# Row norms in groups, scaled in place and stored a tile later, between the mixers and the out-projection of a hybrid encoder on one Trainium2 core

## The chip, the core and the metric

The kernel runs on one core of a Trainium2 chip. The metric is the device time in microseconds (us) of one execution. The core's engines are TensorE (PE in the profile, with PEld for its weight loads), VectorE (DVE), ScalarE (ACT), GpSimd (POOL) and SyncE (SP, which issues most of the DMAs). Each engine runs its own list of instructions in order, and waits where an instruction needs something of another engine or of a DMA.

## The reference

A layer of an encoder: a norm, one projection whose columns go to four mixers, an out-projection with a residual, then a mixture of sixteen experts and a gate. The lines that matter here, cut:

```python
def rmsnorm(x, w):
    xf = x.astype(jnp.float32)
    y = xf * lax.rsqrt(jnp.mean(xf * xf, axis=-1, keepdims=True) + EPS)
    return (y * w.astype(jnp.float32)).astype(x.dtype)
...
def mamba2_mixer(...):
    ...
    y = (y_f + y_b + xs * d_skip[:, None]).reshape(nb, L, GROUP_W)
    return rmsnorm(y * jax.nn.silu(z), norm_w)
...
def hyena_mixer(...):
    ...
    return rmsnorm(y * x0, norm_w)
...
        mixed = jnp.concatenate([retention_mixer(...), mamba2_mixer(...),
                                 hyena_mixer(...), gdn_mixer(...)], axis=-1)
        h = h + jnp.einsum('bln,nd->bld', mixed, w_out[i])
        h = h + expert_choice_moe(rmsnorm(h, norm_ffn_w[i]), router_w[i], ...)
        gate = jax.nn.sigmoid(jnp.einsum('bld,de->ble', rmsnorm(h, ple_norm_w[i]), ple_gate_w[i]))
        h = h + gate * jnp.einsum('blk,kd->bld', p[i], ple_proj_w[i])
    return rmsnorm(h, final_norm_w)
```

SEQ is 1024, D_MODEL 1024, and each mixer gives 256 columns (GROUP_W). All arrays are float32.

## The kernel before

The sequence is worked in eight tiles of 128 tokens (partitions), and in this part of the program from tile 7 down to tile 0. First come the in-projection and the four mixers; then the out-projection and the routing; then sixteen experts, whose weights stream from memory the whole time.

Products are made in three parts: a float32 tile is split into a rounded high part and the rest. For weights, `chunk` loads a block of 128x1024 into `raw`, makes `wh` (the high part, on ScalarE, L1617 or L1620) and `wl` (what is left, by a subtraction, L1618 or L1622). Chunks 1 and 2 of the out-projection's weights also carry the norm weights of the state-space and hyena mixers (L1617, L1618, on VectorE); chunks 0 and 3 do not, and their subtraction (L1622) is put on GpSimd by `pool=c in (0, 3)`. For activations, `rows_T` transposes a tile on TensorE (L1635, tile `tk`), copies the high part on ScalarE (L1636, `xh`) and subtracts on VectorE (L1637, `xl`). `mm3` then issues three matmuls for each pair (L1646 to L1648, tile `ga`). `rw` holds the router's weights, which eight GpSimd instructions scale by a norm weight (L1673).

The end of the mixers is three lists of steps that `weave` interleaves:

- Retention, `attend` and `finish`, a tile ahead of each other: ScalarE's queue loads `rr` (L1445, two buffers), VectorE makes `rqh` (L1447, one buffer), TensorE transposes both (L1451, L1456), ScalarE copies them (L1453 `rqk_`, L1458 `rqt`), TensorE multiplies (L1464 scores, L1468 and L1469 outputs), VectorE masks the scores (L1465, `rS`). `finish` centres and scales the heads: sums and means on VectorE (L1475, L1476, L1478), squares on ScalarE (L1480), a sum (L1481), the root on GpSimd (L203, L204, `rgs`), then L1483, and L1485 writes the result into `rU`, which stays in on-chip memory. The load of `rr` of one tile goes into the buffer of the tile two before, which L1485 of that tile reads last.
- The state-space mixer: `combine` makes `sy` (two buffers): L1061 and L1064 on GpSimd, L1064, L1065 and L1068 on VectorE.
- Hyena: `y` holds all eight tiles; L1393 makes the last product of each.

The rows of `sy` and of `y` are normed by `norm_store`, one tile at a time: a square with its sum on ScalarE (L1086, into `njk`), the root on GpSimd (L203, L204, `nss`, 128x1), a scaling from `y` into `njk` on ScalarE (L1088), and a store of `njk` to the DRAM array MX (L1089), issued from ScalarE's queue. `njk` has two buffers. The out-projection loads 768 columns of a tile back from MX (tile `a`).

Tiles come from pools. `sb2` holds the tiles of the state-space mixer and retention; when it is closed, `sb3`, with the out-projection's `wl3`, `a4`, `xh` and `xl`, opens where it lay, and a tile waits for the tile whose place it takes (`reuse_waits="tile"`). The tile `w4`, which takes the high part of chunk 3, lies where hyena's `y` lay. The order of instructions on each engine is set by a list scheduler with a timeline of its own, not by the order in the source.

## Time and profile before

| | us |
|---|---|
| runs | 1656.79, 1653.63, 1647.57 |
| median of the runs | 1653.63 |
| profiled execution | 1651.48 |
| its span, first to last instruction | 1649.6 |
| PE / DVE / ACT / POOL busy in the span | 1513.7 / 1195.3 / 862.2 / 559.0 |

The mean granted TensorE clock is 0.959 of its upper level of 2.4 GHz. Times in the rows count from the span's start. An engine's busy share is an average over stages with different limits, so the rows below go by stages: the mixers end and the out-projection begins between 690 and 740 us, the out-projection runs to some 860 us, and the experts follow.

### The profile page before, as it was taken

Reading aid. Unit: us, or ns where it says so; the run is one execution under the profiler, and the core shown is the slowest. Engines: PE = TensorE matmul, PEld = TensorE weight load, DVE = VectorE, ACT = ScalarE, POOL = GpSimd, SP = SyncE. Lnnn points to the kernel's source line nnn. Section 1 sums busy time; section 2 is a strip of 40 time slices with the busy share of each in tenths; the row PEclk is TensorE's granted clock in tenths of the full one; section 3 lists DMA queues with packets and bytes.
Section 4 is the critical chain, followed back from the end, with each engine's and each line's share of the span. In section 5 each row is a group of like instructions: output and inputs, shape, how many; then the busy total and the mean of one; then the engine's idle time right before and its main releaser. Section 6 shows DMA issues by size and latency. Waiting matters only on the chain.

```text
span 1649.6 us, 25979 instructions
## 1 busy us (share of the span) xinstructions
PE 1513.7 (92%) x9148; PEld 1251.9 (76%) x9148; DVE 1195.3 (72%) x2060; ACT 862.2 (52%) x1413; POOL 559.0 (34%) x778
## 2 busy tenths in 40 slices
PE   4999999999999899779997999999898999999997
PEld 4877778988778776568875787886676688787886
DVE  5589876942556477955778797998888887777673
ACT  6255342123444335433223776887776767676662
POOL 3126665672865068462223110111111021121121
PEclk9999999999999899869997999999999999999999
DMA  5213557454545485154345999999999988888771
GB/s 182 61 39 96 168 155 243 131 161 105 166 122 167 139 288 163 55 181 156 135 154 214 359 337 363 317 339 350 349 355 336 348 294 295 293 310 303 236 276 52
DMA packets 200671, 362.53 MB, mean 220 GB/s; under 512 B 62046, under 2 KB 124732, under 8 KB 200285
## 3 DMA queue, kind: packets, MB, share of 16 engines
q1 hardware_dynamic: 169016, 296.13, 52.2%
q0 software_dynamic: 12400, 42.29, 8.5%
q10 hardware_dynamic: 19125, 22.45, 4.0%
q8 instruction: 72, 1.18, 0.3%
q14 instruction: 58, 0.48, 0.1%
HBM read 301.04 MB, written 59.77 MB: 219 GB/s over the span
## 4 chain that ended last, share of the span: by engine, by line
PE 45%; DMA 18%; DVE 17%; issue 8%; POOL 6%; ACT 5%; SPq 0%; POOLq 0%; ACTq 0%; DVEq 0%
PE pj L300 8%; DVE wl L1622 6%; PE pj L318 5%; PE ga L1646 4%; DMA raw<-in_exp_w_gate_dram 4%; PE ga L1648 4%; PE ga L1647 4%; DMA raw<-in_exp_w_up_dram 3%; ACT wh L1620 2%; POOL prm L1208 2%; POOL prr L1208 2%; PE pj L1647 2%; PE pj L1646 2%; PE pj L1648 2%; DMA RT<-mo 2%
## 5 line engine op out<-in xcount | busy, mean ns | idle before, releaser
L1622 DVE TENSOR_TENSOR wl<-raw,wh 128x1024 fp32r<-128x1024 f32 x340 | 408.3, 1223 | 86.2 <-ACT wh L1620 83.6
L1620 ACT CAST wh<-raw 128x1024 fp32r<-128x1024 f32 x344 | 356.4, 1052 | 139.1 <-DMA raw<-in_exp_w_up_dram 46.1
L1647 PE MATMUL ga<-wl,xh 128*128 128x512 f32 x512 | 206.4, 403 | 6.8 <-DVE wl L1622 6.7
L1648 PE MATMUL ga<-wh,xl 128*128 128x512 f32 x480 | 189.8, 396 | 0.0
L1646 PE MATMUL ga<-wh,xh 128*128 128x512 f32 x480 | 177.2, 407 | 10.0 <-ACT wh L1620 9.7
L1647 PEld LDWEIGHTS ga<-wl,xh 128*128 128x128 f32 x512 | 98.1, 192 | 34.7 <-DVE wl L1622 15.9
L318 PE MATMUL pj<-wh,hnh 128*128 128x256 f32 (+1 forms) x384 | 113.0, 295 | 7.9 <-DVE zss L915 4.6
L300 PE MATMUL pj<-hnh,wh 128*128 128x512 f32 x288 | 118.4, 411 | 0.8 <-ACT cin L337 0.8
L1646 PEld LDWEIGHTS ga<-wh,xh 128*128 128x128 f32 x480 | 90.6, 191 | 34.9 <-ACT wh L1620 16.5
L300 PE MATMUL pj<-hnl,wh 128*128 128x512 f32 x288 | 117.0, 406 | 0.0
L2009 POOL DMA_INDIRECT H<-b,pidx x15 | 35.4, 2357 | 240.6 <-ACT b L2008 213.7
L300 PE MATMUL pj<-hnh,wl 128*128 128x512 f32 x288 | 116.7, 405 | 0.0
L318 PE MATMUL pj<-wl,hnh 128*128 128x256 f32 (+1 forms) x384 | 110.5, 288 | 0.0
L318 PE MATMUL pj<-wh,hnl 128*128 128x256 f32 (+1 forms) x384 | 110.5, 288 | 0.0
L1647 PE MATMUL pj<-wl,hh 128*128 128x512 f32 x256 | 103.8, 406 | 4.1 <-DVE wl L1622 4.1
L1648 PEld LDWEIGHTS ga<-wh,xl 128*128 128x128 f32 x480 | 91.8, 191 | 18.1
L1648 PE MATMUL pj<-wh,hl 128*128 128x512 f32 x256 | 100.1, 396 | 0.0
L1956 POOL DMA_INDIRECT a<-HN,pidx x16 | 29.9, 1871 | 200.0 <-PE pj L1647 66.4
L1646 PE MATMUL pj<-wh,hh 128*128 128x512 f32 x256 | 89.9, 397 | 0.2 <-ACT hh L1636 0.2
L318 PEld LDWEIGHTS pj<-wh,hnh 128*128 128x128 f32 x384 | 74.4, 194 | 10.4 <-issue 4.1
L346 DVE SCALAR_TENSOR_TENSOR cacc<-cin,pcolh,cacc 128x1024 f32<-128x1024 f32 x48 | 64.8, 1349 | 15.6 <-POOL prm L1208 7.0
L318 PEld LDWEIGHTS pj<-wl,hnh 128*128 128x128 f32 x384 | 74.3, 193 | 0.5 <-issue 0.3
(540 smaller groups left out, 3751.6 us busy)
## 6 DMA issues: line engine op xcount, KB each, us to landing
raw<-in_exp_w_down_dram SPq DMA_DIRECT2D x128, 512.0 KB
raw<-in_exp_w_gate_dram SPq DMA_DIRECT2D x108, 512.0 KB
raw<-in_exp_w_up_dram SPq DMA_DIRECT2D x104, 512.0 KB
wraw<-in_w_in_dram SPq DMA_DIRECT2D x30, 512.0 KB
g<-WD SPq DMA_DIRECT2D x16, 768.0 KB
room<-in_exp_w_up_dram SPq DMA_DIRECT2D x24, 512.0 KB
WD<-gB SPq DMA_DIRECT2D x16, 640.0 KB
room<-in_exp_w_gate_dram SPq DMA_DIRECT2D x18, 512.0 KB
```

What stands on the lines that cost most here:

```text
L300: self.on_pj = nc.tensor.matmul(pj, lhsT=A[:, kt], rhs=B[:, kt, hs], start=i == 0, stop=i == 23)
L318: self.on_pj = nc.tensor.matmul(pj, lhsT=A[:, kt, ts], rhs=B[:, kt, :], start=i == 0, stop=i == 23)
L346: nc.vector.scalar_tensor_tensor(acc, cin[:, 2 - r + j:2 - r + j + 1024], w[j], acc, op0=OP.mult, op1=OP.add)
L1208: tt = lambda o, a, b, op: nc.gpsimd.tensor_tensor(out=o, in0=a, in1=b, op=op)
L1620: nc.scalar.copy(h, r)
L1622: e.tensor_tensor(out=l, in0=r, in1=h.bitcast(F32), op=OP.subtract)
L1646: nc.tensor.matmul(ps, lhsT=xh[:, k], rhs=wh[:, hs], start=first, stop=False)
L1647: nc.tensor.matmul(ps, lhsT=xh[:, k], rhs=wl[:, hs], start=False, stop=False)
L1648: return nc.tensor.matmul(ps, lhsT=xl[:, k], rhs=wh[:, hs], start=False, stop=last)
L1956: self.fetched = self.nc.gpsimd.indirect_dma_start(out=xg, out_offset=None, in_=self.HN if src is None else src, in_offset=bass.IndirectOf ...
L2009: nc.gpsimd.indirect_dma_start(out=self.H, out_offset=bass.IndirectOffsetOnAxis(ap=idx[:, :1], axis=0), in_=y, in_offset=None, compute_op= ...
```

## The change

Three things are changed.

**The norms.** `norm_store` becomes two steps. `norms(ys)` squares a group of rows into `njk` (only as a place to put the squares), and takes one root for the group on GpSimd. `store` then scales a row in place, in `y` or `sy` itself, and issues its store to MX from there. The state-space mixer calls `store` for a tile after the next tile has been combined; hyena groups its tiles as (7, 6), (5, 4, 3, 2), (1, 0), with a `yield` between the norms and the stores of a group. `nss` has four buffers and not two.

**The subtractions.** `pool=c in (0, 3)` is dropped, so that the weight subtractions of chunks 0 and 3 run on VectorE too. The eight scalings of `rw` become one instruction on VectorE over 128x128.

**The places.** The tiles `sbT`, `smv`, `sxb`, `sdec`, `sST` are the first to be laid into `sb2`, and `wl3`, `a4`, `xh`, `xl` the first into `sb3`.

```diff
+    def pcs(self, name, n):
+        j = self.col[name]
+        return self.PC[:, j:j + n]
...
     def ssm(self):
         nc, a = self.nc, self.a
         T2 = self.t2
+
+        T2([128, 256], "sbT", 2)
+        T2([128, 4, 128], "smv", 3)
+        T2([128, 4, 128], "sxb", 2)
+        T2([128, 4, 64], "sdec")
+        ST = T2([128, 8, 4, 2, 64], "sST")
...
-        ST = T2([128, 8, 4, 2, 64], "sST")
...
-            self.norm_store(y, t, 256)
-
-        E = weights(NT - 1)
+            return self.norms([y]), 0, y, t, 256
+
+        E, made = weights(NT - 1), None
         for t in range(NT - 1, -1, -1):
             if t < NT - 1:
                 backward(t)
             p = products(t)
             En = weights(t - 1) if t else None
-            combine(t, E, *p)
+            done, made = made, combine(t, E, *p)
+            if done:
+                self.store(*done)
             E = En
             yield
-
-    def norm_store(self, y, t, col):
-
-        nc = self.nc
-        s = self.t4([128, 2], "nss", 2)
-        jk = self.t4([128, 256], "njk", 2)
-        nc.scalar.activation(jk, y, AF.Square, accum_out=s[:, 0:1])
-        self.rsqrt(s[:, 1:2], s[:, 0:1], 1.0 / 256, EPS)
-        nc.scalar.activation(jk, y, AF.Copy, scale=s[:, 1:2])
-        nc.scalar.dma_start(self.MX[t][:, col:col + 256], jk)
-
+        self.store(*made)
+
+    def norms(self, ys):
+
+        nc = self.nc
+        n = len(ys)
+        s = self.t4([128, 2, 4], "nss", 4)
+        for i, y in enumerate(ys):
+            jk = self.t4([128, 256], "njk", 2)
+            nc.scalar.activation(jk, y, AF.Square, accum_out=s[:, 0, i:i + 1])
+        self.rsqrt(s[:, 1, 0:n], s[:, 0, 0:n], 1.0 / 256, EPS)
+        return s
+
+    def store(self, s, i, y, t, col):
+
+        nc = self.nc
+        nc.scalar.activation(y, y, AF.Copy, scale=s[:, 1, i:i + 1])
+        nc.scalar.dma_start(self.MX[t][:, col:col + 256], y)
...
-        for t in range(NT - 1, -1, -1):
-            nc.vector.tensor_tensor(out=y[:, t], in0=y[:, t], in1=x0[(7 - t) // 2][:, t % 2], op=OP.mult)
-            self.norm_store(y[:, t], t, 512)
+        for ts in ((7, 6), (5, 4, 3, 2), (1, 0)):
+            for t in ts:
+                nc.vector.tensor_tensor(out=y[:, t], in0=y[:, t], in1=x0[(7 - t) // 2][:, t % 2], op=OP.mult)
+            s = self.norms([y[:, t] for t in ts])
+            yield
+            for i, t in enumerate(ts):
+                self.store(s, i, y[:, t], t, 512)
             yield
...
         w = {}
+
+        for n, dt, bufs in (("wl3", F32R, 6), ("a4", F32, 2), ("xh", F32R, 2), ("xl", F32R, 2)):
+            self.t3([128, 1024], n, bufs, dt=dt)
...
-            w[c] = self.chunk(a["w_out"][0], c, pool=c in (0, 3), norm=(None, "ssm_norm_w", "hy_norm_w", None)[c],
+            w[c] = self.chunk(a["w_out"][0], c, norm=(None, "ssm_norm_w", "hy_norm_w", None)[c],
                               first=2 * c, **own)
         rw = self.t5([128, 8, NE], "rw")
         nc.sync.dma_start(rw, a["router_w"][0].rearrange("(k p) e -> p k e", p=128))
-        for k in range(8):
-            nc.gpsimd.tensor_scalar(rw[:, k], rw[:, k], self.pc("norm_ffn_w", k), None, op0=OP.mult)
+        nw8 = self.pcs("norm_ffn_w", 8)
+        nc.vector.tensor_tensor(out=rw, in0=rw, in1=nw8[:, :, None].to_broadcast([128, 8, NE]), op=OP.mult)
```

The scheduler turns this into another order on the engines. The lists below are the instruction lists of both kernels at three places; the line numbers after are those of the new source (L1447 of before is L1469 after, L1465 is L1487, L1481 is L1503, L1618 is L1640, L1622 is L1644, L1637 is L1659).

VectorE, at the end of the mixers, before:

```order
731 L1485 TENSOR_TENSOR rU<-ro,rr 128x256
732 L1465 TENSOR_TENSOR rS<-sp,rdm 128x2x128 x2
733 L1618 SCALAR_TENSOR_TENSOR wl_7057<-raw_7055,pcol,wh_7056 128x1024
734 L1618 SCALAR_TENSOR_TENSOR wl_7063<-raw_7061,pcol,wh_7062 128x1024
735 L1618 SCALAR_TENSOR_TENSOR wl_7081<-raw_7079,pcol,wh_7080 128x1024
736 L1618 SCALAR_TENSOR_TENSOR wl_7087<-raw_7085,pcol,wh_7086 128x1024
737 L1447 TENSOR_TENSOR rqh<-rr,rpw 128x512
738 L1475 TENSOR_REDUCE rgs<-sp 128x4
739 L1476 TENSOR_SCALAR rgs<-rgs 128x4
740 L1478 TENSOR_TENSOR ro<-sp,rgs 128x256
741 L1637 TENSOR_TENSOR xl<-tk,xh 128x512
```

and after:

```order
732 L1469 TENSOR_TENSOR rqh<-rr,rpw 128x512
733 L1500 TENSOR_TENSOR ro<-sp,rgs 128x256
734 L1640 SCALAR_TENSOR_TENSOR wl_7050<-raw_7048,pcol,wh_7049 128x1024
735 L1640 SCALAR_TENSOR_TENSOR wl_7056<-raw_7054,pcol,wh_7055 128x1024
736 L1644 TENSOR_TENSOR wl_7062<-raw,wh_7061 128x1024
737 L1644 TENSOR_TENSOR wl_7068<-raw,wh_7067 128x1024
738 L1640 SCALAR_TENSOR_TENSOR wl_7074<-raw_7072,pcol,wh_7073 128x1024
739 L1640 SCALAR_TENSOR_TENSOR wl_7080<-raw_7078,pcol,wh_7079 128x1024
740 L1503 TENSOR_REDUCE rgs<-sp 128x4
741 L1698 TENSOR_TENSOR rw<-rw,pcol 128x128
742 L1644 TENSOR_TENSOR wl_7085<-raw,w_7043 128x1024
743 L1644 TENSOR_TENSOR wl_7090<-raw,w_7043 128x1024
```

Before, `rqh` and the steps L1475 to L1478 follow the four subtractions L1618, and the first `xl` follows them directly; after, `rqh` and the steps come first, then six subtractions, L1503, the scaling of `rw`, two more subtractions, and then `xl`.

GpSimd, at the last tile of the state-space mixer (`rgs` is the root of retention, `nss` of the norms), before:

```order
456 L1061 TENSOR_TENSOR sy<-sxT,dsk 128x256
457 L1064 TENSOR_TENSOR sy<-sy,sy_6986 128x256
458 L203 TENSOR_SCALAR nss<-nss 128x1
459 L204 TENSOR_TENSOR nss<-nss,mhalf 128x1
460 L203 TENSOR_SCALAR nss<-nss 128x1
461 L204 TENSOR_TENSOR nss<-nss,mhalf 128x1
462 L203 TENSOR_SCALAR rgs<-rgs 128x4
463 L204 TENSOR_TENSOR rgs<-rgs,mhalf 128x4
```

and after:

```order
455 L207 TENSOR_SCALAR nss<-nss 128x4
456 L208 TENSOR_TENSOR nss<-nss,mhalf 128x4
457 L1070 TENSOR_TENSOR sy<-sxT,dsk 128x256 x2
458 L1073 TENSOR_TENSOR sy<-sy,sy_6923 128x256
459 L1073 TENSOR_TENSOR sy<-sy,sy_6992 128x256
460 L207 TENSOR_SCALAR rgs<-rgs 128x4
461 L208 TENSOR_TENSOR rgs<-rgs,mhalf 128x4
```

The first products of the last two `sy` (L1061 before, L1070 after) now stand together behind the root of four hyena tiles, and the next `rgs` behind both of them.

ScalarE, around the load of `rr` for tile 4 (L1445 before, L1467 after), before:

```order
551 L1086 ACTIVATE njk,nss<-y_5869 128x256
552 L1086 ACTIVATE njk,nss<-sy 128x256
553 L1458 COPY rqt<-sp 128x512
554 L1088 ACTIVATE njk<-y_5869,nss 128x256
555 L1445 DMA rr<-RT 128x1024
556 L1089 DMA MX<-njk 128x256
557 L1088 ACTIVATE njk<-sy,nss 128x256
```

and after:

```order
548 L1100 ACTIVATE njk,nss<-sy 128x256
549 L1107 ACTIVATE sy<-sy,nss 128x256
550 L1100 ACTIVATE njk,nss<-sy 128x256
551 L1100 ACTIVATE njk,nss<-y_5873 128x256
552 L1108 DMA MX<-sy 128x256
553 L1100 ACTIVATE njk,nss<-y_5873 128x256
554 L1467 DMA rr<-RT 128x1024
555 L1107 ACTIVATE sy<-sy,nss 128x256
556 L1108 DMA MX<-sy 128x256
```

After, the squares of the last two `sy` and of the last two `y` all stand ahead of this load; before, it stands between two tiles' norms.

## Rows read from the trace of the kernel before

**Rows 1.** The busy times of each engine in stretches of 10 us from the span's start; the columns are the stretch, its length, then busy us and instructions of PE, PEld, DVE, ACT and POOL, TensorE's granted clock, the DMA share and GB/s.

```profile
700.00:710.00 10.00, 5.37 (x26) 4.68 (x26) 5.54 (x16) 4.92 (x15) 7.46 (x14) 0.50 0.33 109
710.00:720.00 10.00, 8.00 (x33) 6.84 (x34) 5.75 (x8) 3.81 (x11) 6.47 (x10) 0.50 0.73 222
720.00:730.00 10.00, 5.05 (x20) 4.19 (x20) 8.11 (x9) 3.17 (x9) 9.49 (x16) 0.50 0.80 282
730.00:740.00 10.00, 10.00 (x45) 7.56 (x44) 2.88 (x6) 2.95 (x9) 2.84 (x5) 0.90 0.40 123
740.00:750.00 10.00, 10.00 (x59) 8.61 (x59) 4.11 (x9) 3.91 (x6) 5.98 (x4) 1.00 0.54 167
820.00:830.00 10.00, 9.76 (x58) 8.28 (x57) 9.48 (x43) 2.50 (x6) 3.44 (x15) 1.00 0.53 184
```

**Rows 2.** The waits from 690 to 760 us: engine, what waits, what ended it; total us, times, the longest.

```profile
POOL nss L203 <- ACT njk L1086: 11.6, 6, 3.6
ACT njk L1086 <- DMA MX<-njk: 11.3, 5, 3.3
...
PE sp L1456 <- DVE rqh L1447: 4.9, 1, 4.9
```

**Rows 3.** The chain of work that ended last, followed back from 735 us: start, duration, engine and line.

```profile
705.45 1.84 DMA MX<-njk
...
710.26 3.99 DMA MX<-njk
...
716.98 8.62 DVE wl L1618 x4
```

**Rows 4.** The timeline of VectorE (DVE) from 697 to 745 us: start, duration, line, operation, tiles, sizes and count; in brackets the idle time before it and what ended that.

```profile
699.53 0.41 DVE L1393 TENSOR_TENSOR y<-y,hF 128x256 f32<-128x256 f32 x1
...
704.06 0.41 DVE L1485 TENSOR_TENSOR rU<-ro,rr 128x256 f32<-128x256 f32 x1
...
713.42 0.43 DVE L1485 TENSOR_TENSOR rU<-ro,rr 128x256 f32<-128x256 f32 x1
...
716.90 8.71 DVE L1618 SCALAR_TENSOR_TENSOR wl<-raw,pcol,wh 128x1024 fp32r<-128x1024 f32 x4
725.53 0.68 DVE L1447 TENSOR_TENSOR rqh<-rr,rpw 128x512 f32<-128x512 f32 x1
...
727.16 0.68 DVE L1637 TENSOR_TENSOR xl<-tk,xh 128x512 fp32r<-128x512 f32 x1
```

**Rows 5.** The timeline of GpSimd (POOL) over the same stretch.

```profile
706.00 0.61 POOL L1061 TENSOR_TENSOR sy<-sxT,dsk 128x256 f32<-128x256 f32 x1 [0.62 <-ACT njk L1088]
706.69 0.73 POOL L1064 TENSOR_TENSOR sy<-sy,sy 128x256 f32<-128x256 f32 x1
...
711.91 1.02 POOL L204 TENSOR_TENSOR rgs<-rgs,mhalf 128x4 f32<-128x4 f32 x1
...
716.46 5.65 POOL L1622 TENSOR_TENSOR wl<-raw,wh 128x1024 fp32r<-128x1024 f32 x2
...
724.55 3.56 POOL L1673 TENSOR_SCALAR rw<-rw,pcol 128x16 f32<-128x16 f32 x7
...
741.98 4.77 POOL L1622 TENSOR_TENSOR wl<-raw,w 128x1024 fp32r<-128x1024 f32 x2 [2.07 <-ACT w L1620]
```

**Rows 6.** The timeline of ScalarE over the same stretch; ACTq is its queue, which issues DMAs.

```profile
706.61 0.33 ACTq L1445 DMA_DIRECT2D rr<-RT  x1
707.31 0.42 ACT L1086 ACTIVATE njk<-y 128x256 f32<-128x256 f32 x1 [1.38 <-DMA MX<-njk]
...
708.76 0.51 ACT L1088 ACTIVATE njk<-y,nss 128x256 f32<-128x256 f32 x1 [0.46 <-POOL nss L204]
...
713.64 0.42 ACT L1086 ACTIVATE njk<-y 128x256 f32<-128x256 f32 x1 [1.31 <-DMA MX<-njk]
...
715.77 0.33 ACTq L1445 DMA_DIRECT2D rr<-RT  x1
...
719.78 0.42 ACT L1086 ACTIVATE njk<-y 128x256 f32<-128x256 f32 x1 [2.65 <-DMA MX<-njk]
```

**Rows 7.** The timeline of TensorE (PE) over the same stretch; the ends of matmuls are modelled, so that neighbours overlap and the spacing of starts is the pace.

```profile
710.62 1.09 PE L1451 MATMUL sp<-ident,rr 128*128 128x128 f32 x4 [3.04 <-DMA rr<-RT]
...
715.30 1.22 PE L1464 MATMUL sp<-rqk__7244 64*128 64x128 f32 x4 [1.38 <-ACT rqt L1458]
716.45 0.69 PE L1468 MATMUL sp<-rr,rS 128*128 128x64 f32 x2
...
717.35 0.64 PE L1468 MATMUL sp<-rr,rS 128*128 128x64 f32 x2
...
726.35 1.09 PE L1456 MATMUL sp<-ident,rqh 128*128 128x128 f32 x4 [4.95 <-DVE rqh L1447]
...
727.66 0.63 PE L1647 MATMUL ga<-wl,xh 128*128 128x512 f32 x1
728.09 0.63 PE L1646 MATMUL ga<-wh,xh 128*128 128x512 f32 x1
```

**Rows 8.** First the page's group of the weight subtractions on VectorE over the whole program (line, operation, tiles, count | busy us, mean ns | idle before); then the four L1618 of the stretch (duration min/median/max in ns); then a stretch of 200 us of the experts, with the columns of the stretches above.

```profile
L1622 DVE TENSOR_TENSOR wl<-raw,wh 128x1024 fp32r<-128x1024 f32 x340 | 408.3, 1223 | 86.2 <-ACT wh L1620 83.6
...
L1618 DVE SCALAR_TENSOR_TENSOR wl<-raw,pcol,wh x4: 1272/2146/3372, 716.9 to 724.3; 128x1024 fp32r<-128x1024 f32 x4
...
1000.00:1200.00 200.00, 189.85 (x881) 147.06 (x880) 174.41 (x192) 149.75 (x170) 29.93 (x10) 1.00 0.95 338
```

## Prediction

> **What bounds the kernel now.** I read the busy times by stage first, and only the join between mixers and out-projection matters here: TensorE is busy 5.37, 8.00 and 5.05 of 10 us from 700 to 730, at the half clock (0.50), and from 730 on it is full, at full clock from 740, up to about 820 [rows 1]. In that full stretch an edit that only shortens another engine's work gains nothing; in the join a us by which TensorE's steady work starts earlier or later goes to the end about one for one, because the experts behind it run with the DMA at 0.95 and prefetch only as buffers come free [rows 8].
>
> The waits of 690 to 760 show two things of equal size on the side that the change is about: ScalarE waits 11.3 us in five pieces for a store from `njk` to land, and GpSimd waits 11.6 us for ScalarE's squares [rows 2]. But the wait on TensorE's side is another: 4.9 us for `rqh` [rows 2]. The chain of waits tells why. It passes through two landings of MX<-njk, 1.84 and 3.99 us, and then through four weight subtractions on VectorE, 8.62 us, before `rqh` of tile 4 is made at 725.53 and TensorE restarts at 726.35 [rows 3, 4, 7]. So the bound is VectorE's order: `rqh`(4) stands behind the four subtractions, while the late stores of `njk`, at 719.78 and behind, hold up ScalarE and nobody else [rows 6].
>
> **The subtractions.** Four (chunks 0 and 3) go from GpSimd to VectorE. On GpSimd two took 5.65 us and two 4.77 [rows 5]; VectorE takes 1.22 each over the whole program [rows 8]. Four by 1.22 is 4.9 us more on VectorE. The scaling of `rw` is an 8-piece chain on GpSimd (seven in 3.56 us [rows 5]) and becomes one VectorE instruction on 128x128, half the elements of the 128x256 product of 0.41 us [rows 4]: 0.25 us, an estimate. Something comes back: the four L1618 took 8.62 us together, from 1.27 for the quickest to 3.37 for the slowest [rows 3, 8], and they ran while GpSimd did its own two, 716.46 to 722.1 [rows 5]. At 1.27 each they need 5.1 us, so 3.5 us return if GpSimd's work beside them is what stretched them. I take that, since the only rows of the same shape at 1.2 us are those with GpSimd idle; the other end, 8.6 us, goes into the range. The Trainium skill (GPSIMD Engine Reference, section 1, Specifications) says that GpSimd shares its SBUF interfaces with VectorE, with contention when VectorE has two SBUF inputs; the spread just named fits it, and no run here yet shows it alone. By that rule the stretch goes for certain; without it eight subtractions would cost the sum up to 3.5 us more.
>
> **The norms.** Sixteen roots on 128x1 become fewer and wider ones, and each scaled row is written in place and stored from `y` or `sy`, not from `njk`. What is removed from ScalarE is the 11.3 us of waits for landings; its work (a square 0.42, a scaling 0.51, an issue 0.33 us) stays in number [rows 6]. Of the five waits, two (1.38 us at 707.31 and 1.31 us at 713.64) stand ahead of the issue of `rr` of tile 4 at 715.77, the other three behind it [rows 6]. Only the first two, 2.7 us, can bring `rr`(4) earlier.
>
> What is added is a wait in another place. `sy` has two buffers; so the first product of `sy` of tile 1 on GpSimd (L1061) now waits until the store of tile 3 has landed, and tile 0 until that of tile 2. Queued behind these two on GpSimd is the root for tile 6 of retention, then on VectorE L1483 and L1485 of tile 6, and then, on ScalarE, the issue of `rr`(4). Its squares of the last rows stand ahead of that issue too. The nearest rows for a landing are 1.84 and 3.99 us [rows 3]. The Trainium skill (DMA: Bandwidth & Descriptors, the anatomy of one DMA) puts the fixed part of a transfer at about 2.0 us, most of it until the last byte is confirmed, and only then the semaphore fires: it speaks against holding a work buffer until its store is through, and by it 131 KB would take about 2.3 us, an estimate that lies between the two rows.
>
> I place this by hand with the row durations. The last `y` product stays at 699.5, and L1485 of tile 7 about 703 to 704 [rows 4]; the stores of `sy` 3 and 2 are issued at about 706.6, about where before has the issue that the chain names at 705.45 [rows 3], and two squares and a scaling more stand ahead of it now; they land at 708 to 708.5 with 1.84 us. Two L1061 by 0.61 and two L1064 by 0.73 [rows 5] make 2.7: 710.8. The root for tile 6, 0.2 and 1.02 [rows 5]: 712.1. On VectorE some six `sy` steps, one L1465 and L1483, each on 128x256 and about 0.42 us, stand between from 711 on, so that L1485 of tile 6 runs at 714.4, where before has it at 713.42 [rows 4]. `rr`(4) is issued at 716.0, after the last squares (before 715.77), and takes 4.0 us as the one issued at 706.61 and used at 710.62 did [rows 6, 7]: 720.0. So the 2.7 us that ScalarE saves are spent again on GpSimd.
>
> **The order on VectorE.** Now `rqh`(4) stands ahead of the subtractions: made at 720.6, and the mean step of tile 5 at 721.0. That takes away the 4.9 us wait as such. But the subtractions no longer start at 716.9; they wait on the same queue for `rr`(4). Six of them (four by 1.27, two by 1.22: 7.5 us) end at 728.5. L1481 of tile 5 (0.42) and `rw` (0.25) follow, then two more subtractions (2.4): 731.6; then L1465 and the first `xl`, which starts at 732.0, where before it starts at 727.16 [rows 4]. That is the sum's main term: the first `xl` is 4.9 us late. TensorE loses less than that: ahead of VectorE's eighth subtraction it does four L1456, four L1464, four out-projection products and one pair of L1468 and L1469. At the full clock these are half of what the rows at the half clock show by their lengths and their spacing, 0.43, 0.65, 0.92 and 0.45 [rows 7]: 2.45 us of the work that before does from 726.35 on. Its steady work starts at 731.9 with 2.45 us already done, against 726.35: 5.55 - 2.45 = **+3.1 us**. If the two L1468 groups of tile 4, which need L1465 from behind the eight subtractions, hold the rest, it starts at 733.6, +4.8. I take the middle, **+4 us**; after it TensorE is full to 820 [rows 1] and nothing gives it back. The lower end is an order in which `rr`(4) is issued five us sooner, which would make 3.1 - 5.1 = -2 us.
>
> The free time that GpSimd gets costs and gains nothing: 4.77 of its 10.4 us of subtractions lie at 742 [rows 5], where TensorE is full. The placement of the first tiles costs nothing that I can find: the first writes of the out-projection on the old places (L1618 at 716.90) follow directly on VectorE's own instruction, with no wait for a buffer [rows 4].
>
> **The rivals.**
> - *A, forecast:* norms no longer wait, but the first `xl` and with it TensorE wait for `rr`(4), `rqh`(4) and eight subtractions in a row. +4 us: 1651.5 + 4 = 1655.5 profiled.
> - *B, faster:* ScalarE's landings were the bound [rows 2]; the whole join moves up by 8 to 11 us. For it: the chain does pass through two of them [rows 3]. Against: only 2.7 of 11.3 us stand ahead of `rr`(4). It decides if `rr`(4) is issued by about 708. 1653.6 - 10 = 1643.
> - *C, slower:* the in-place stores hold `sy` for 4 us or more instead of 1.84, since four of `y` and two of `sy` are issued together while the DMA share climbs to 0.73 and 0.80 [rows 1]. Each us goes through the two L1061, the root of tile 6, `rr`(4) and `rqh`(4) one for one, and the cast of chunk 3 into `w`, laid on `y`, waits for the last `y` stores, with `xh` of tile 7 behind it. Two landings of 3.99 instead of 1.84 add 2.2 to 4.3, a slow `rr` 2: about +10, 1653.6 + 10 = 1664. It decides from a landing above some 3 us. The same happens if the eight subtractions stay at 2.1 us.
> - *D, no effect:* the changed order balances out: `rqh` early, `xl` late, 1653.6.
>
> **How the numbers follow.** The profiled run lasted 1651.48 us, of which the span is 1649.6; the median of the three runs is 2.15 us above it, and the runs lie between 1647.6 and 1656.8. The sum is made against the profiled run (1655.5) and put on the median: **1657.5 us**. A 0.56, B 0.14, C 0.24, D 0.06. A reaches from -2 (1651.6) to +8 (1661.6). For 8 in 10 the range takes in A and D, most of C and part of B: 1645 to 1668. A measurement of this kernel can tell about 0.5%, or 8.3 us, from no change; faster by more is only B's, 0.14; slower by more than that is C and the upper edge of A, 0.25; the rest is 0.61.
>
> **What the profile after would show.** Right: no wait of ScalarE for MX<-njk; GpSimd's L1061 waiting for MX<-sy; `rqh`(4) at about 720 and ahead of the subtractions; these at 1.2 to 1.3 us each; the first `xl` at 730 to 734; TensorE full from 732 to 734. Wrong: `rr`(4) issued before 712 (B); the subtractions at 2 us although GpSimd is idle (no contention); TensorE losing time after 740, where I have nothing; or the shift of the join being taken up by the experts, so that the end stands where it was.

## The result, and the profile after

| | before | after |
|---|---|---|
| median of 7 runs, us | 1653.63 | 1663.76 |
| lowest, highest | 1647.57, 1657.0 | 1659.44, 1667.61 |
| profiled execution, span | 1649.6 | 1662.3 |
| mean granted TensorE clock | 0.959 | 0.954 |

The ratio is 1.0061, with a 95% interval of 1.0040 to 1.0082: the changed kernel is some 10 us slower. A second measurement (below, h4) gave 1.0051 (1.0030 to 1.0071). The forecast was 1657.5 us, in a range of 1645 to 1668.

The join in the stretches of [rows 1], after:

```profile
700.00:710.00 10.00, 8.61 (x38) 8.11 (x38) 6.10 (x18) 7.43 (x23) 4.96 (x11) 0.50 0.08 27
710.00:720.00 10.00, 5.83 (x25) 4.56 (x23) 5.93 (x15) 4.14 (x11) 5.51 (x9) 0.50 0.66 191
720.00:730.00 10.00, 4.49 (x19) 3.53 (x18) 5.33 (x8) 5.09 (x14) 2.07 (x7) 0.50 0.90 284
730.00:740.00 10.00, 8.36 (x26) 6.39 (x27) 8.87 (x13) 2.09 (x4) 3.45 (x2) 0.50 0.78 277
740.00:750.00 10.00, 10.00 (x46) 8.22 (x46) 2.08 (x3) 0.58 (x1) 0.00 (x0) 0.96 0.21 83
```

TensorE's last gap ends at 733.48, where before it ends at 726.35 [rows 7], and its granted clock is 0.50 up to 740 us, where before it is 0.50 up to 732. Next, two of the waits from 690 to 760 us:

```profile
DVE rqh L1469 <- DMA rr<-RT: 9.3, 3, 4.7
...
PE sp L1473 <- DMA rr<-RT: 6.2, 2, 3.1
```

ScalarE's wait for MX<-njk [rows 2] is gone, as forecast. The largest waits that concern the join are now for `rr`, on VectorE and on TensorE. VectorE's timeline, which answers to [rows 4]:

```profile
699.16 0.92 DVE L1498 TENSOR_SCALAR rgs<-rgs 128x4 f32<-128x4 f32 x1
...
701.93 0.41 DVE L1500 TENSOR_TENSOR ro<-sp,rgs 128x256 f32<-128x256 f32 x1
...
703.60 0.41 DVE L1503 TENSOR_REDUCE rgs<-sp 128x4 f32<-128x256 f32 x1
...
704.27 0.41 DVE L1412 TENSOR_TENSOR y<-y,hF 128x256 f32<-128x256 f32 x1
...
713.24 0.69 DVE L1469 TENSOR_TENSOR rqh<-rr,rpw 128x512 f32<-128x512 f32 x1 [2.29 <-DMA rr<-RT]
...
719.33 0.41 DVE L1507 TENSOR_TENSOR rU<-ro,rr 128x256 f32<-128x256 f32 x1
...
725.26 0.69 DVE L1469 TENSOR_TENSOR rqh<-rr,rpw 128x512 f32<-128x512 f32 x1 [2.31 <-DMA rr<-RT]
...
726.21 2.47 DVE L1640 SCALAR_TENSOR_TENSOR wl<-raw,pcol,wh 128x1024 fp32r<-128x1024 f32 x2
728.60 2.35 DVE L1644 TENSOR_TENSOR wl<-raw,wh 128x1024 fp32r<-128x1024 f32 x2
730.87 2.47 DVE L1640 SCALAR_TENSOR_TENSOR wl<-raw,pcol,wh 128x1024 fp32r<-128x1024 f32 x2
...
733.79 2.35 DVE L1644 TENSOR_TENSOR wl<-raw,w 128x1024 fp32r<-128x1024 f32 x2
...
736.40 0.68 DVE L1659 TENSOR_TENSOR xl<-tk,xh 128x512 fp32r<-128x512 f32 x1
```

Read it from the last `y` product (704.27, L1412 after, L1393 before): `rqh` of tile 5 waits 2.29 us, L1507 of tile 6 runs at 719.33, `rqh` of tile 4 waits again and stands at 725.26, and then eight subtractions run one after the other, two in 2.35 to 2.47 us, up to the first `xl` at 736.40. GpSimd and ScalarE over the same stretch, as in [rows 5, 6]:

```profile
713.66 1.31 POOL L1070 TENSOR_TENSOR sy<-sxT,dsk 128x256 f32<-128x256 f32 x2 [3.12 <-DMA MX<-sy]
...
733.76 2.43 POOL L207 TENSOR_SCALAR rgs<-rgs 128x4 f32<-128x4 f32 x1 [10.93 <-DVE rgs L1503]
```

```profile
709.54 0.87 ACTq L1108 DMA_DIRECT2D MX<-sy  x2
...
720.53 0.33 ACTq L1467 DMA_DIRECT2D rr<-RT  x1
...
728.44 1.99 ACT L1642 CAST w<-raw 128x1024 fp32r<-128x1024 f32 x2 [1.16 <-DMA MX<-y]
```

GpSimd's two products of `sy` wait 3.12 us for the stores of `sy` that ScalarE issued from 709.54. `rr` of tile 4 is issued at 720.53. And the cast of chunk 3 into `w` waits for the stores from `y`, with `rqt` and the first `xh` in the queue behind it. The chain of waits goes through that cast (start, duration, and for an instruction the tile that it writes and its line):

```profile
723.38 4.88 DMA MX<-y
...
728.44 1.99 ACT w L1642 x2
730.43 0.49 ACT rqt L1480
...
730.97 1.22 PE sp L1486 x4
...
732.85 0.59 ACT xh L1658
```

and TensorE, which answers to [rows 7], begins its steady work there; the first product with `xl` (L1670) is at 738.26:

```profile
730.97 1.22 PE L1486 MATMUL sp<-rqk__7353 64*128 64x128 f32 x4 [2.52 <-ACT rqt L1480]
...
733.48 0.80 PE L1668 MATMUL ga<-wh,xh 128*128 128x512 f32 x1 [0.67 <-ACT xh L1658]
...
738.26 0.78 PE L1670 MATMUL ga<-wh,xl 128*128 128x512 f32 x1
```

### The profile page after: what moved, and what is told of

Same layout as the page of the kernel before. It is cut to its first block, busy times and chain, and to the rows that moved or that the text cites. A ratio compares the mean times of both kernels' runs of the same rounds, so it can differ in the third digit from the quotient of the medians.

```text
span 1662.3 us, 25964 instructions
## 1 busy us (share of the span) xinstructions
PE 1522.7 (92%) x9148; PEld 1258.2 (76%) x9148; DVE 1193.3 (72%) x2065; ACT 859.4 (52%) x1413; POOL 537.0 (32%) x756
## 3 DMA queue, kind: packets, MB, share of 16 engines
q1 hardware_dynamic: 169016, 296.13, 51.9%
## 4 chain that ended last, share of the span: by engine, by line
PE 28%; DMA 10%; DVE 8%; issue 5%; ACT 4%; POOL 1%; POOLq 0%; ACTq 0%; DVEq 0%
PE ga L1670 5%; PE ga L1668 5%; PE ga L1669 5%; DVE wl L1644 5%; DMA raw<-in_exp_w_gate_dram 4%; DMA raw<-in_exp_w_up_dram 3%; ACT wh L1642 3%; PE pj L1669 2%; PE pj L1668 2%; PE pj L1670 2%; DMA raw<-in_exp_w_down_dram 1%; PE sp L1657 1%; PE pj L1747 1%; DMA a<-H,tidx 1%; PE tk L1670 1%
## 5 line engine op out<-in xcount | busy, mean ns | idle before, releaser
L1644 DVE TENSOR_TENSOR wl<-raw,wh 128x1024 fp32r<-128x1024 f32 x342 | 410.4, 1222 | 90.0 <-ACT wh L1642 87.3
L1670 PE MATMUL ga<-wh,xl 128*128 128x512 f32 x480 | 189.0, 394 | 0.0
L1670 PEld LDWEIGHTS ga<-wh,xl 128*128 128x128 f32 x480 | 91.0, 190 | 18.0
L1670 PE MATMUL pj<-wh,hl 128*128 128x512 f32 x256 | 100.2, 396 | 0.0
```

What stands on the lines that cost most here:

```text
L1644: e.tensor_tensor(out=l, in0=r, in1=h.bitcast(F32), op=OP.subtract)
L1670: return nc.tensor.matmul(ps, lhsT=xl[:, k], rhs=wh[:, hs], start=False, stop=last)
```

## The experiments

Two theories stood against each other at first. **A**, that of the prediction: the order on VectorE (`rqh` of tile 4 first, then the subtractions, then `xl`) and the held `sy` lengthen the join. **B**, a rival: ScalarE's waits for landings were the bound, so that freeing them should have helped. Others came up on the way: that the places make a wait, that the subtractions cost as such, and that only the grouping counts. Line numbers are those of each kernel's own source. The ratios below are to the kernel before, run on the same chip.

| run | what it is | ratio (95% interval) |
|---|---|---|
| e1 | changed, places as before | 1.0068 (1.0043 to 1.0094) |
| e2 | changed, norms as before | 1.0018 (1.0000 to 1.0037) |
| e3 | changed, subtractions and `rw` on GpSimd | 1.0054 (1.0032 to 1.0076) |
| e4 | changed, four buffers of `sy` | 1.0086 (1.0061 to 1.0111) |
| f1 | changed, six subtractions ahead of `rqh` | 1.0036 (1.0015 to 1.0058) |
| f2 | changed, stores from a tile of their own | 1.0048 (1.0033 to 1.0064) |
| f3 | before, four buffers of `njk` | 1.0041 (1.0018 to 1.0064) |
| f4 | before again | one profile |
| h1 | before, scaled in place, nothing else | 1.0007 (0.9988 to 1.0027) |
| h2 | before, subtractions put into the gaps | 1.0008 (0.9986 to 1.0029) |
| h3 | before, four `njk` and subtractions in the gaps | 1.0077 (1.0049 to 1.0105) |
| h4 | changed, again | 1.0051 (1.0030 to 1.0071) |

**e1, the places.** Both blocks of first allocations are removed; the order of instructions on every engine is the changed kernel's.

```diff
-        T2([128, 256], "sbT", 2)
-        T2([128, 4, 128], "smv", 3)
...
-        for n, dt, bufs in (("wl3", F32R, 6), ("a4", F32, 2), ("xh", F32R, 2), ("xl", F32R, 2)):
-            self.t3([128, 1024], n, bufs, dt=dt)
```

> The changed kernel without its third part: the first tiles are laid where they lay before; every engine's instruction order is that of the changed kernel. Theory A (the order on VectorE and the held sy cost the time): no change from the changed kernel, 1.006 of the kernel before (1.004 to 1.008), about 1663 us. Rival (the places make a wait): most of the 10 us comes back, 0.999 to 1.002.

1.0068: no change from the changed kernel. The places cost nothing and bring nothing.

**e2, without the new norms.** `norms`, `store` and the groups are replaced by `norm_store` of before; subtractions and places stay changed.

```diff
-            return self.norms([y]), 0, y, t, 256
+            self.norm_store(y, t, 256)
```

> The changed kernel with the norms of before (one tile at a time, through njk): six subtractions stand ahead of rqh of tile 4, two behind the first xl. Theory A: the subtractions start at about 717 as before and need 7.4 us at 1.24 each, so that rqh of tile 4 comes about a us earlier and xl follows directly: 0.998 to 1.001. Rival (the subtractions on VectorE cost as such, 5 us of work on an engine that is full at the end of the mixers): 1.003 or more.

1.0018: by the medians some 5 to 8 us of the loss go with the norms (against h4, the changed kernel and e1). What is left, 0 to 0.37%, lies between the two expectations; the join itself doesn't show it (table further down).

**e3, without the move of the subtractions.**

```diff
-            w[c] = self.chunk(a["w_out"][0], c, norm=...
+            w[c] = self.chunk(a["w_out"][0], c, pool=c in (0, 3), norm=...
...
-        nc.vector.tensor_tensor(out=rw, in0=rw, in1=nw8[:, :, None].to_broadcast([128, 8, NE]), op=OP.mult)
+        for k in range(8):
+            nc.gpsimd.tensor_scalar(rw[:, k], rw[:, k], self.pc("norm_ffn_w", k), None, op0=OP.mult)
```

> The changed kernel with the subtractions of chunks 0 and 3 and the scaling of rw back on GpSimd: rqh of tile 4 first, then four subtractions, then xl. Theory A: the first xl waits for four subtractions and not eight, 5.1 us if GpSimd leaves them at 1.27 each and 8.6 us if it stretches them, where the changed kernel needs 9.9: 1.3 to 4.8 us less, 1.003 to 1.005. Rival (only the norms, the held sy and its store, cost the time): no change, 1.006.

1.0054, a little over what A expected; the interval holds A's upper end and the rival's 1.006, so the ratio doesn't decide. VectorE's four subtractions took 1.27 to 1.29 us each, since GpSimd's own lay ahead of and behind them. The first `xl` came 1.7 us sooner after the last `y` product than in the changed kernel (30.4 against 32.1 us), but the first product with `xl` did not (34.3 against 34.0). So the number of subtractions on VectorE is not what costs the time.

**e4, four buffers of `sy`.**

```diff
-            y = T2([128, 256], "sy", 2)
+            y = T2([128, 256], "sy", 4)
```

> The changed kernel with four buffers of sy and not two, so that the last two products on GpSimd (L1070) don't wait for a store of sy to land (3.12 us in the profile of the changed kernel). If that wait sets when rr of tile 4 is issued, the join comes 3 to 5 us earlier: 1.003 to 1.004. Rival (rr of tile 4 is late because VectorE ended the last y product 4.7 us later than before): no change, 1.006.

Neither: 1.0086, slower. The wait for MX<-sy is gone, but the scheduler, given the buffers, puts the work of the last state-space tiles further ahead on VectorE, and the last `y` product comes at 709.1, 60.3 us after the last `hA` product where before needs 51.1. The run doesn't isolate the wait, and tells nothing of its cost.

**f1, the subtractions ahead of `rqh`.** In `attend`, with `self.subs` the list of the subtractions in the order of `chunk`; `self.after` has the scheduler issue what stands under it behind the instructions named:

```diff
-            nc.vector.tensor_tensor(out=qh, ...
+            with self.after(*(self.subs[:6] if t == 4 else ())):
+                nc.vector.tensor_tensor(out=qh, ...
```

> The changed kernel with one order imposed: rqh of tile 4 is issued on VectorE behind the six subtractions of chunks 1, 0 and 2, and everything else stands as in the changed kernel. If the subtractions waiting for rqh are what makes the first xl late (profile of the changed kernel: subtractions from 726.2, first xl at 736.4, while the step before rqh was done at 723), they start 3.4 us sooner and the first xl comes about 3 us sooner: 1.003 to 1.005 of the kernel before. Rival (the stores that hold sy and y set the pace, the order on VectorE does not): no change, 1.006 to 1.007, or more, since rqh of tile 4 comes 5 us later.

1.0036, as A expected; but the interval overlaps that of the changed kernel. Three rows of its VectorE timeline:

```profile
700.06 0.42 DVE L1412 TENSOR_TENSOR y<-y,hF 128x256 f32<-128x256 f32 x1
...
719.21 2.47 DVE L1641 SCALAR_TENSOR_TENSOR wl<-raw,pcol,wh 128x1024 fp32r<-128x1024 f32 x2
...
729.66 0.69 DVE L1661 TENSOR_TENSOR xl<-tk,xh 128x512 fp32r<-128x512 f32 x1
```

The subtractions start 19.2 us after the last `y` product (21.9 in the changed kernel) and the first `xl` is there after 29.6 (32.1). The first product with `xl` is only 1.8 us sooner (32.2 against 34.0), because TensorE now waits 4.1 us for `xh`, which again stands behind the cast that waits for MX<-y, and does retention's tile 4 later.

**f2, stores from a tile of their own.**

```diff
-        nc.scalar.activation(y, y, AF.Copy, scale=s[:, 1, i:i + 1])
-        nc.scalar.dma_start(self.MX[t][:, col:col + 256], y)
+        jk = self.t2([128, 256], "njs", 4)
+        nc.scalar.activation(jk, y, AF.Copy, scale=s[:, 1, i:i + 1])
+        nc.scalar.dma_start(self.MX[t][:, col:col + 256], jk)
```

> The changed kernel with the scaled rows written into a tile of their own (four buffers) and stored from there, not in place: neither sy nor y is held by a store. Grouping and the later store stay; on VectorE six subtractions now stand ahead of rqh of tile 4, as without the new norms. If the in-place stores are the cause (GpSimd waits 3.1 us for MX<-sy, the cast of chunk 3 on ScalarE 1.2 us for MX<-y with rqt and xh queued behind it), the time is that of the changed kernel without the new norms: 1.000 to 1.003. Rival (groups with one root, or the store a tile later, are the cause): 1.005 or more.

1.0048: only a part comes back, if any. With nothing held, the cast of chunk 3 runs at 714.3 with no wait, all subtractions follow at 716.2, and the first `xl` is there 27.5 us after the last `y` product, as in the kernel before (27.6). And still TensorE stands idle, for another reason. SyncE's queue and TensorE's timeline:

```profile
717.74 0.42 SPq L1709 DMA_DIRECT2D a<-MX  x1
```

```profile
724.55 0.69 PE L1658 MATMUL tk<-ident,a 128*128 128x128 f32 x2 [6.61 <-DMA a<-MX]
```

The load of tile 7's rows (`a`) is issued at 717.74, 18.6 us after the last `y` product (before: 11.4), when the DMA engines are busy (a share of 0.95 in 720 to 730), and TensorE waits for it until 724.55. So the two holds are not the whole cost of the new norms: without them another chain is as late.

**f3, four buffers of `njk` on the kernel before.** The tile moves to `sb2`, where there is room for it.

```diff
-        jk = self.t4([128, 256], "njk", 2)
+        jk = self.t2([128, 256], "njk", 4)
```

> The kernel before with four buffers of njk and not two: ScalarE's 11.3 us of waits for MX<-njk go, and nothing else of the change is made. Case B of the prediction (these waits were the bound): 8 to 11 us faster, 0.993 to 0.995. My theory (they were not; four subtractions on VectorE and rr of tile 4 bound the join): 0.998 to 1.002, whatever order the scheduler now chooses.

1.0041: B falls, since with ScalarE's waits for MX<-njk gone the kernel gets slower and not 8 to 11 us faster. The order on VectorE changed with it, so f3 does not price these waits at the order of before. My own expectation of no change was wrong too. VectorE's timeline shows how:

```profile
720.64 0.69 DVE L1447 TENSOR_TENSOR rqh<-rr,rpw 128x512 f32<-128x512 f32 x1 [0.46 <-DMA rr<-RT]
...
723.53 11.21 DVE L1618 SCALAR_TENSOR_TENSOR wl<-raw,pcol,wh 128x1024 fp32r<-128x1024 f32 x4
...
735.33 0.68 DVE L1637 TENSOR_TENSOR xl<-tk,xh 128x512 fp32r<-128x512 f32 x1
```

`rqh` of tile 4 is made at 720.64, 5 us sooner than before, but the four subtractions now stand behind it, run from 723.53 beside GpSimd's, and take 11.21 us; the first `xl` is at 735.33, where it was at 727.16 [rows 4].

**f4, the kernel before again**, for its profile.

> The kernel before once more, for a second profile: if the shifts that I read between two profiles outside the join (up to 3 us at 637, where TensorE's clock rises at another time, and 4 to 7 us in the experts) are those of single executions, this profile differs from the first by as much there, and by under 1 us from the last y product to the first xl. If they belong to the change, it agrees with the first to under 1 us everywhere.

From 636 to 640 and from 900 to 1000 us, the columns of [rows 1]; first the profile before:

```profile
636.00:640.00 4.00, 4.00 (x22) 3.32 (x22) 3.47 (x4) 0.07 (x1) 3.92 (x5) 0.94 0.03 6
900.00:1000.00 100.00, 97.69 (x509) 79.07 (x508) 87.68 (x114) 74.64 (x94) 15.13 (x12) 1.00 0.94 344
```

then the same kernel again:

```profile
636.00:640.00 4.00, 4.00 (x12) 2.87 (x12) 2.58 (x3) 0.23 (x1) 3.77 (x4) 0.50 0.00 0
900.00:1000.00 100.00, 97.67 (x502) 79.13 (x502) 88.60 (x116) 74.66 (x94) 15.13 (x12) 1.00 0.94 346
```

and the changed kernel:

```profile
636.00:640.00 4.00, 4.00 (x14) 3.12 (x13) 3.58 (x5) 0.60 (x1) 4.00 (x5) 0.50 0.00 0
900.00:1000.00 100.00, 94.97 (x497) 76.49 (x498) 82.22 (x122) 65.44 (x83) 15.13 (x12) 0.96 0.90 322
```

The half clock of 636 to 640 appears in one execution of the kernel before and not in the other, and it shifts the rest by 2.15 us; so the 2 us that the changed kernel loses there (matching instructions start 3.18 us later behind it and 1.2 ahead of it) are not its own. From the last `hA` product to the first product with `xl` the two profiles of before agree: 81.2 and 81.0 us. At the end of the program they are 0.1 us apart: the second execution gave the 2.15 us back, 0.7 of them by 770 and 1.4 behind 843, where the changed kernel lost another 3.3 us.

**h1, in place and nothing else**, on the kernel before:

```diff
-        nc.scalar.activation(jk, y, AF.Copy, scale=s[:, 1:2])
-        nc.scalar.dma_start(self.MX[t][:, col:col + 256], jk)
+        nc.scalar.activation(y, y, AF.Copy, scale=s[:, 1:2])
+        nc.scalar.dma_start(self.MX[t][:, col:col + 256], y)
```

> The kernel before with one thing of the norms changed: each row is scaled in place and stored from y or sy at once, tile by tile, with no groups, no later store, and the subtractions and places of before. On VectorE rqh of tile 4 now stands ahead of the four subtractions and the retention steps of tile 6 ahead of the last y product, as with all of the new norms. If the order that follows from the held buffers is the cause, this alone costs most of what the new norms cost: 1.003 to 1.006. Rival (grouping and the later store are the cause): 0.999 to 1.002.

1.0007: the rival is right about this. The order on VectorE is the one that I blamed, `rqh` of tile 4 ahead of four subtractions and retention's steps ahead of the last `y` product:

```profile
703.17 0.41 DVE L1393 TENSOR_TENSOR y<-y,hF 128x256 f32<-128x256 f32 x1
...
722.59 2.22 DVE L1447 TENSOR_TENSOR rqh<-rr,rpw 128x512 f32<-128x512 f32 x1 [2.57 <-DMA rr<-RT]
724.73 6.99 DVE L1618 SCALAR_TENSOR_TENSOR wl<-raw,pcol,wh 128x1024 fp32r<-128x1024 f32 x4
...
732.31 0.68 DVE L1637 TENSOR_TENSOR xl<-tk,xh 128x512 fp32r<-128x512 f32 x1
```

and yet the whole time is as before within the interval, which ends at 1.0027. So scaling in place, and the order that the scheduler makes of it, costs under 4.5 us when it comes without groups and without the later store. That it costs nothing is not shown: in h1's one profile the join loses 3.0 us (table below).

**h2 and h3, the subtractions put into VectorE's gaps**, on the kernel before and on f3; in h3 the same edit with four `njk`.

```diff
-            nc.vector.tensor_tensor(out=qh, ...
+            with self.after(*(self.subs[0:2] if t == 5 else ())):
+                nc.vector.tensor_tensor(out=qh, ...
...
-            nc.vector.tensor_tensor(out=o, in0=o, in1=s[:, 3]...
+            with self.after(*(self.subs[4:6] if t == 6 else ())):
+                nc.vector.tensor_tensor(out=o, in0=o, in1=s[:, 3]...
```

> The kernel before with an order imposed on VectorE: the four L1618 go into its idle gaps behind the last y product, two ahead of rqh of tile 5 and two ahead of L1483 of tile 6, so that rqh of tile 4 no longer waits for them. They are over before GpSimd starts its own two at 716, so 1.27 us each. If VectorE's order of ready subtractions and waiting retention steps is what bounds the join, TensorE's steady work starts 3 to 5 us sooner: 0.997 to 0.998. Rival (retention's chain through rr, which gets 2 to 3 us later, sets the pace): 1.000 to 1.004.

> Four buffers of njk on the kernel before, with the same imposed order (two L1618 ahead of rqh of tile 5, two ahead of L1483 of tile 6). Four buffers alone gave 1.004 with the subtractions from 723.5 and the first xl at 735.3. If that loss was the subtractions standing behind rqh of tile 4, it goes: 0.996 to 1.000. Rival (the loss came with the freer ScalarE in another way): 1.003 or more.

1.0008 and 1.0077: the rivals, both times. In h2 the first `xl` does come sooner (24.8 us after the last `y` product, 27.6 before), but TensorE pays for it at `rqh` of tile 5 and at the `rqt` that follows:

```profile
714.68 1.09 PE L1452 MATMUL sp<-ident,rr 128*128 128x128 f32 x4 [2.98 <-DMA rr<-RT]
718.22 1.09 PE L1457 MATMUL sp<-ident,rqh 128*128 128x128 f32 x4 [2.46 <-DVE rqh L1448]
...
727.98 1.22 PE L1465 MATMUL sp<-rqk__7244 64*128 64x128 f32 x4 [6.90 <-ACT rqt L1459]
```

In h3 `rr` of tile 4 is issued only at 729.4, and TensorE waits 12.9 us in one piece, for the load of `a`. Neither beats the kernel before.

**h4, the changed kernel again.**

> The changed kernel once more, on the chip of the other runs here: 1.004 to 1.009 of the kernel before. Its profile tells what belongs to the change and what to one execution: from the last y product to the first product with xl 33.5 to 34.5 us (30.1 before), from the last hA product at 650 to the last y product 52 to 54 us (51.1 before), and in the experts a loss between 0 and 7 us.

1.0051. VectorE's last `y` product and its first `xl` are 32.07 us apart, as in the first profile (32.13), and the three stretches named above came out as expected: 33.8, 53.1 and a loss of 2.8 us in the experts.

**The join of all profiles**, worked out from their timelines: from the last `hA` product (near 650) to the last `y` product, from there to the first `xl` on VectorE and to the first product with it on TensorE; and, matching each TensorE instruction with that of before, how much its shift has grown since 650, at 770 and at 843 us of before.

| run | `hA` to `y` | `y` to `xl` | `y` to product | loss at 770 | loss at 843 |
|---|---|---|---|---|---|
| before, before again | 51.1, 51.2 | 27.6, 27.3 | 30.1, 29.8 | 0, -0.7 | 0, -0.7 |
| after, h4, e1 | 52.6, 53.1, 53.6 | 32.1, 32.1, 32.2 | 34.0, 33.8, 34.0 | 4.2, 4.4, 4.8 | 6.3, 6.5, 6.9 |
| e2 | 51.6 | 27.9 | 31.3 | 0.4 | 0.4 |
| e3 | 52.6 | 30.4 | 34.3 | 3.5 | 7.2 |
| e4 | 60.3 | 28.0 | 30.1 | 8.8 | 10.5 |
| f1 | 54.2 | 29.6 | 32.2 | 4.8 | 6.8 |
| f2 | 51.7 | 27.5 | 32.7 | 4.9 | 7.0 |
| f3 | 51.7 | 35.8 | 37.9 | 8.5 | 8.4 |
| h1 | 53.1 | 29.1 | 33.5 | 3.0 | 3.0 |
| h2 | 50.7 | 24.8 | 28.8 | 0.0 | 0.0 |
| h3 | 51.9 | 32.1 | 35.9 | 9.3 | 12.8 |

The kernels that lose 6 us or more by 843 have ratios of 1.0036 and more; those that lose 3 us or less have 1.0018 and less. So most of the loss that the ratios show is made ahead of 843.

Not all of that is waiting. From 770 to 824 TensorE is busy for 9.7 us or more of every 10 before and after, and yet the shift grows by 3.0 to 3.2 us there in after, h4, e1, e3, e4, f1, f2 and h3, and by 0.1 us or less in the others; some 1.1 us of it come back by 843. (In e3 and h3 a stretch at clock 0.50 near 838 adds 1.7 us.) TensorE's own order tells how. Before, the eight score products of a retention tile (L1464) stand together; after, they stand in two groups of four (L1486) with other work between, and four take as long as eight. Before:

```profile
776.53 0.72 PE L1464 MATMUL sp<-rqk__7749 64*128 64x128 f32 x8
```

and after:

```profile
784.21 0.71 PE L1486 MATMUL sp<-rqk__7735 64*128 64x128 f32 x4
...
789.43 0.71 PE L1486 MATMUL sp<-rqk__7735 64*128 64x128 f32 x4
```

From the start of each such group to that of the next instruction, the last four tiles take 2.61 us before and 5.11 us after; of the 3.2 us, the score products make 1.9. The groups of four stand there in every kernel in which the shift grows so, and h3, which has the norms of before, is among them: they belong to the order that the scheduler made. No run changes this order alone.

## Why the prediction was right in sign and short in size

- **The stage and the path were right.** Most of the loss arises in the join, and ScalarE's waits that were to go went. The likeliest case, slower by 4 us, was right in sign; its size was less than half of the 10 us. At 770, behind the join, TensorE had lost 4.2, 4.4 and 4.8 us (after, h4, e1), where +3.1 to +4.8 was forecast.
- **The hand-placed chain held, step by step, when counted from the last `y` product** (the forecast, then the two profiles of the changed kernel): L1507 of tile 6 14.9, then 15.1 and 15.0; `rr` of tile 4 issued 16.5, then 16.3 and 16.2; `rqh` of tile 4 21.1, then 21.0 and 20.9; the first `xl` 32.5, then 32.1 and 32.1. The subtractions took 1.22 and 1.28 us, as assumed; TensorE's first product with `xl` came 3.9 and 3.7 us later than before.
- **The step that failed first is "the last `y` product stays at 699.5".** From the last `hA` product it comes 1.6 us later in the changed kernel, 2.1 in h4 and 2.5 in e1. The order shows why: L1498, L1500 and L1503 of retention's tile 6 (0.92, 0.41 and 0.41 us in the rows above) now stand ahead of it on an engine that is full there. I had compared the orders only behind that product. That the loss at 770 still came out as forecast is in part luck: the late `y` is in it, so what follows `y` cost less than the sum had.
- **The second is "after it TensorE is full to 820 and nothing gives it back".** The prediction took a full TensorE to do the same work in the same time, and named time lost after 740 as a sign of being wrong. It was lost: 2.1 us more between 770 and 843 in after, h4 and e1, where the score products in groups of four alone take 1.9 us longer.
- **Behind the join the shift does not go to the end one for one.** At the end it stands at 12.7 us in the first profile, 8.6 in h4 and 13.2 in e1, from 9.5, 5.8 and 7.2 at 843: the experts lost 2.8 to 6.0 us more. In 900 to 1000 the changed kernel moved 322 GB/s where both profiles of before moved 344 and 346. What does that is open, and it need not be the change's own: h2, without any part of the change, moved 331 GB/s and its shift grew by 6.9 us there, though its ratio is 1.0008; e2's grew by 7.0 us, from 3.6 to 10.6, at 1.0018, and e3's shrank by 1.5. Both profiles of before are also of executions 1 to 4 us below that kernel's medians (1651.5 and 1651.6 against 1652.7 to 1655.6), which every shift at the end contains.
- **Rival C gave the right time (1664) in part by the right mechanism.** Its condition was met: landings took over 3 us, and the cast into `w` waited for MX<-y with `xh` behind it, 4.88 us in the chain. But its other half did not cost: the stores of `sy` were issued 5.3 us after the last `y` product and not 7.1, which made up for the longer landing. And the holds are not the whole cause: h1 has both buffers written in place and its whole time shows no clear loss; f2 holds neither and loses 0.48%. So that 1664 met the measured 1663.76 is largely luck.
- **Rival B** is refuted by f3 as far as the scheduler's order goes with the edit, **rival D** by the intervals of the two measurements. That the places are no wait was right (e1).
- **The move of the subtractions costs nothing that can be told.** They were a large term of the sum, eight in a row ahead of the first `xl`. With four fewer (e3) the first `xl` is 1.7 us sooner, but the loss is 3.5 us at 770 against 4.2, and 7.2 at 843 against 6.3. That the stretch of the four L1618 goes with GpSimd's share was right. The prediction's reason for it was not exact: the two that took 1.29 and 1.27 us did not have GpSimd idle beside them, but at short work that took 1.15 us (L1673 on 128x16, at 722.24) and 0.99 us (L203 on 128x1, at 723.47). The Trainium skill (GPSIMD Engine Reference, section 1, Specifications) has the two engines contend for their shared SBUF interfaces when VectorE has two SBUF inputs; f3 and the changed kernel show such a slowdown, as told below.
- **My explanation by the order on VectorE alone fell.** `rqh` of tile 4 ahead of the subtractions makes the first `xl` late wherever it stands (changed, e1, e3, f3, h4); but h1 has it and its whole time shows no clear loss, and h2, which undoes what it stands for, gains nothing.
- **What is shown of the cause, and what stays open.** The new norms make 5 to 8 of the 10 us by the medians (e2); groups and the later store without the holds still lose 0.48% (f2); in-place scaling alone costs under 4.5 us (h1, whose profile shows 3.0 in the join). TensorE's order makes some 2 of the 6 to 7 us lost by 843. No run has the groups without the later store. Which single wait is the cause of the rest is not settled: retention's chain through `rr`, the cast behind MX<-y, the load of `a` and the subtractions end within a few us of each other, and each experiment that shortened one met the next.

## What to carry to other kernels

A wait that shows large in the profile of an engine (here 11.3 us of landings) may be the slack that keeps a good order; take it away alone first, and see whether the time moves. Where a scheduler sets the order, an edit in one helper moves work on every engine: compare the orders from well ahead of the stage in question, not only from its last known point, and on the full engine too, whose time for the same instructions can change with their order. And profile the unchanged kernel twice, so that a clock that rises 4 us later in one execution isn't read as the change's doing.

## What the runs showed of the hardware

**VectorE and GpSimd slow each other.** A subtraction of 128x1024 takes VectorE 1.22 to 1.28 us with GpSimd idle (726.2 to 733 in the changed kernel). In f3, where the two engines ran theirs side by side, the duration on each (min/median/max in ns) was:

```profile
L1618 DVE SCALAR_TENSOR_TENSOR wl<-raw,pcol,wh x4: 1273/3368/3435, 723.5 to 731.3; 128x1024 fp32r<-128x1024 f32 x4
```

```profile
L1622 POOL TENSOR_TENSOR wl<-raw,wh x2: 3327/3332/3338, 723.7 to 727.0; 128x1024 fp32r<-128x1024 f32 x2
```

GpSimd needs 2.33 to 2.37 us for the same with VectorE idle (h2, h3). In the changed kernel a GpSimd instruction on 128x4 that takes 0.2 us took 2.43 us (733.76 above) while VectorE ran two subtractions in 2.35 us (733.79).

**Landings took longer where the DMA engines were busier.** The store of 128x256 from `y` took 4.88 us in the chain of the changed kernel, with a DMA share of 0.66 to 0.90 in 710 to 730; before, the two in the chain, issued at 705.45 and 710.26, took 1.84 and 3.99 us [rows 3], with a share of 0.33 in 700 to 710 and 0.73 in 710 to 720 [rows 1]. The Trainium skill (DMA: Bandwidth & Descriptors, the anatomy of one DMA) gives, for transfers that GpSimd issues, about 2.0 us as the fixed part and would have made it 2.3 with the bytes, an estimate; the measured time decides, and it is twice that here, for a store from ScalarE's queue.

**Four small products took as long as eight.** At the full clock eight score products (64 rows) in one group took 0.65 us up to the start of the next instruction, and four took 0.64 us (776.53 before, 784.21 after); why is not shown here.
